# A hybrid decoder block with expert retrieval: gathered rows paced over the whole dense stage, three buffers for split rows, one-hots moved to ScalarE, unsplit meta columns

## The chip, the cores and the metric

The kernel runs on one core of one Trainium2 chip. The metric is the device time of one execution in microseconds (us), the median of the runs. Engines are named as in the profile: PE is TensorE, DVE is VectorE, ACT is ScalarE, POOL is GpSimd and SP is SyncE; PEld is the load of weights into PE.

## The reference

512 tokens of width 1024, with 16 learned meta tokens in front, go through one layer in float32:

```
h = concat(meta, x)
h = h + hybrid_mixer(rmsnorm(h))      # stick-breaking attention and gated linear attention
h = h + peer_ffn(rmsnorm(h))          # product-key retrieval of experts
return rmsnorm(h)[:, 16:]

def peer_ffn(hn, ...):                # 8 heads, 128 keys a half, top 16, 128 x 128 experts
    s1, s2 = q[:, :, 0] @ sub_keys1, q[:, :, 1] @ sub_keys2
    v1, i1 = top_k(s1, 16);  v2, i2 = top_k(s2, 16)
    sc, pos = top_k(v1[:, None] + v2[None, :], 16)
    e = i1 * 128 + i2 at pos;  g = softmax(sc)          # 128 experts a token
    act = gelu(expert_u[e] . hn)
    y = sum over the 128 experts of g * act * expert_v[e]
```

So each token picks 128 of 16384 experts, each a row of 1024 numbers in `expert_u` and one in `expert_v`.

## The kernel before

**Stages.** `front` norms the input and projects it (w_in in chunks of 256 columns) into queries, keys, values and gates, and runs both attentions; `mid` applies w_out and the second norm and projects the retrieval queries. The projections use float32 operands split into a high and a low part (`hilo`, lines 174 and 175: the high part by ACT, the low part by DVE) and three matmuls per product (`mm3`, lines 179 to 181). The 16 meta columns of keys and gates are products of their own with 16 moving columns, into `pz`, from the same split weights `wh` and `wl` and the split activations `hnh` and `hnl`.

**Look stage.** The tokens lie in four blocks of 128. Three of them (DENSE) are computed against all 16384 experts, the fourth (block 3, GATHER) only against its own. A u row (`u_row`) takes 128 experts: 0.5 MB of `expert_ut` into `uf`, split into `uh` and `ul`, 24 matmuls against the 384 dense tokens, Gelu into `ge`. Between u rows a queue of generators runs the retrieval. For each block `topk` finds experts and gates: scores by PE, copied to `sc` by ACT (line 626), then MAX8, FIND_INDEX8 and MATCH_REPLACE8 on DVE, and two lookups, each of 16 products (line 683) and one sum (line 687). For each dense block `spread` turns them into gates over all experts: 32 steps of four tokens, each with a one-hot `B` (line 769, DVE), a product `Am` of two smaller one-hots (line 771, POOL), four matmuls (line 775, PE), and an eviction `st` with a step of 16 elements (line 776, ACT). `st` goes out to `Gd` in memory. The jobs stand in the order topk 0, spread 0, topk 1, spread 1, topk 2, spread 2, topk 3. The `ge` of the pairs of u rows computed here goes out to `Ad` (23 pairs).

**Dense stage.** The rows go on in pairs. For the pairs that are not yet computed, two more u rows come first (41 pairs); the others are read back from `Ad`. Each pair then takes two v rows (`v_operands`, `v_block`): 0.5 MB of `expert_v` into the same `uf` buffers, split into `uh` and `ul` as above, `ge` times the gates `gt` (1.5 MB of `Gd` for every eight rows) and split into `wh` and `wl`, and 18 matmuls of 512 columns that add up in six banks `acc`. Beside them runs block 3 (`gathered`): 128 times a gather of `expert_u` rows by an indirect DMA from POOL (line 715) into one of six buffers `gu` and a product with accumulation on DVE (line 722), then Gelu on ACT, and 128 gathers of `expert_v` that DVE adds to `y` (line 733).

**What sets the order.** Both stages are paced by a queue: each u row pays 4.2 units, each v row 4.1, times a rate (RATES: 1.3 in the look stage, 0.62 in the dense stage), and each step of a generator costs what it yields (1.0 for four tokens of `spread`, 1.3 for a gathered row). From the program a scheduler then fixes one order for each engine, which the engine follows. The tile pools set the buffers: 4 for `uf`, 2 for `uh` and `ul`, 6 for `gu`, 3 for `B` and `Am`, 6 banks for `sx`.

Of the kernel before, what the change touches and what calls it, by code (L numbers as in the profile page):

```python
# [21 lines left out]
D = 1024  # L22
# [12 lines left out]
GB = 6  # L35
GEB = 5
UF = 4


RATES = (1.3, 0.62)  # L40
LNEXP = "natural_log_exp_and_others"

SEGS = []
# [17 lines left out]
def build(tc, d, out):  # L61
# [121 lines left out]
    def proj(src, c, jobs, act, cols=256, halves=(0, 1)):  # L183


        for half in halves:
            wf = wp.tile([128, 4, 256], F32, name="wf", bufs=WF)
            nc.sync.dma_start(wf[:, :, :cols], src[c, :, half * 4:half * 4 + 4, :cols])
            wh = wp.tile([128, 4, 256], F32R, name="wh", bufs=2)
            wl = wp.tile([128, 4, 256], F32R, name="wl", bufs=2)  # L190
            hilo(wh[:, :, :cols], wl[:, :, :cols], wf[:, :, :cols])
            for (o, kind, w0, w1, t0, t1, fst) in jobs:
                for k in range(4):
                    kt = half * 4 + k
                    a = act(kt, t0, t1)
                    w = (wh[:, k, w0:w1], wl[:, k, w0:w1])
                    l, r = (w, a) if kind == 'f' else (a, w)
                    mm3(o, l, r, kt == 0 and fst, kt == KT - 1)
# [4 lines left out]
                 b % 2 == 0) for b in range(NB)]  # L203

    win = d["w_in"]
    oTh = wp.tile([128, KT, W], F32R, name="oTh")
    oTl = wp.tile([128, KT, W], F32R, name="oTl")

    def front():
# [24 lines left out]
        for q in range(2):  # L234
            for x, n, col in rows:
                t = bank(next(tags))
                for k in range(4):
                    T.transpose(t[:, k * n:(k + 1) * n], x[:, (4 * q + k) * 128:(4 * q + k + 1) * 128], ident[:n, :n])
                for k in range(4):
                    kt = 4 * q + k  # L240
                    hi = hnh[:, kt, col:col + n]
                    A.activation(hi, t[:, k * n:(k + 1) * n], AF.Copy, scale=g1[:, kt:kt + 1])
                    V.scalar_tensor_tensor(hnl[:, kt, col:col + n], t[:, k * n:(k + 1) * n], g1[:, kt:kt + 1],
                                           hi.bitcast(F32), op0=OP.mult, op1=OP.subtract)
        consts_b()

        def act(kt, a, b):
# [2 lines left out]
        def feat(c, meta=None):  # L250
            outs = [pj(), pj()]
            jobs = [(outs[m], 'f', m * 128, (m + 1) * 128, NM, E, True) for m in range(2)]
            if meta is not None:
                jobs += [(meta[:, m * 16:(m + 1) * 16], 'f', m * 128, (m + 1) * 128, 0, NM, m == 0) for m in range(2)]
            proj(win, c, jobs, act)
            return outs

# [134 lines left out]

        def gates_():
            p, pm = pj(), pz()
            proj(win, 12, [(p[:66], 'f', 0, 66, NM, E, True), (pm[:66, :16], 'f', 0, 66, 0, NM, True)], act, cols=66)
            A.activation(glr[:, NM:], p[:16], AF.Copy)
            A.activation(glr[:, :NM], pm[:16, :16], AF.Copy)

# [212 lines left out]
    def topk(blk):  # L611
# [63 lines left out]
        df = mp.tile([128, NH, TK], F32, name="df")  # L675
        V.tensor_copy(df[:, :, 0:1], cs[:, :, 0:1])
        V.tensor_sub(df[:, :, 1:], cs[:, :, 1:], cs[:, :, :TK - 1])
        terms = sc.rearrange("p s h k -> p (s h k)").rearrange("p (a h k) -> p a h k", a=TK, h=NH)

        def lookup(dst, src, keys, op, vals):  # L680

            for a in range(TK):
                V.scalar_tensor_tensor(terms[:, a], src, float(keys[a]), vals[:, :, a:a + 1].to_broadcast([128, NH, TK]),  # L683
                                       op0=op, op1=OP.mult)
                if a % 4 == 3:
                    yield 0.9
            V.tensor_reduce(dst, terms.rearrange("p a h k -> p (h k) a"), op=OP.add, axis=AX.X)

        yield from lookup(cs.rearrange("p h k -> p (h k)"), fp, STARTS, OP.is_ge, df)
        ci = mp.tile([128, 2, NH, TK], I32, name="ci")  # L690
# [44 lines left out]
    def spread(blk, nb=3):  # L735

        pt = bank("sx")
        for i, src in enumerate((sels[blk][:, 0], sels[blk][:, 1], gates[blk])):  # L740
            T.transpose(pt[:, i * 128:(i + 1) * 128], src, ident)
        iT = bp.tile([128, 4, 128], F32, name="iT")
        V.tensor_copy(iT[:, :3], pt[:, :384].rearrange("p (a b) -> p a b", a=3))
        ii = bp.tile([128, 2, 128], I32, name="ii")
        V.tensor_copy(ii[:, 0], pt[:, :128])
        V.tensor_scalar(ii[:, 1], ii[:, 0], 7, None, op0=OP.bitwise_and)
        V.tensor_scalar(ii[:, 0], ii[:, 0], 3, None, op0=OP.logical_shift_right)
        V.tensor_copy(iT[:, 0], ii[:, 0])
        V.tensor_copy(iT[:, 3], ii[:, 1])
        yield 1.5  # L750
        sh = [128, 4, 128]
        io4 = io128.unsqueeze(1).to_broadcast(sh)
        for tb in range(128 // TT):
            st = bp.tile([128, 128, TT], F32, name="st", bufs=2)
            tc_ = slice(tb * TT, (tb + 1) * TT)
            ohu = bp.tile([128, TT, 16], F32, name="ohu", bufs=2)
            V.tensor_tensor(ohu, io128[:, :16].unsqueeze(1).to_broadcast([128, TT, 16]),
                            iT[:, 0, tc_].unsqueeze(2).to_broadcast([128, TT, 16]), op=OP.is_equal)
            ohl = bp.tile([128, TT, 8], F32, name="ohl", bufs=2)
            V.tensor_tensor(ohl, io128[:, :8].unsqueeze(1).to_broadcast([128, TT, 8]),  # L760
                            iT[:, 3, tc_].unsqueeze(2).to_broadcast([128, TT, 8]), op=OP.is_equal)
            V.tensor_tensor(ohl, ohl, iT[:, 2, tc_].unsqueeze(2).to_broadcast([128, TT, 8]), op=OP.mult)  # L762
            yield 1.2
            for t4 in range(TT // 4):
                p = bank("sx")
                c_ = slice(tb * TT + t4 * 4, tb * TT + t4 * 4 + 4)
                l_ = slice(t4 * 4, t4 * 4 + 4)
                B = bp.tile(sh, F32, name="B", bufs=nb)
                V.tensor_tensor(B, io4, iT[:, 1, c_].unsqueeze(2).to_broadcast(sh), op=OP.is_equal)  # L769
                Am = bp.tile(sh, F32, name="Am", bufs=nb)  # L770
                P.tensor_tensor(Am.rearrange("p t (u l) -> p t u l", l=8),  # L771
                                ohu[:, l_].unsqueeze(3).to_broadcast([128, 4, 16, 8]),
                                ohl[:, l_].unsqueeze(2).to_broadcast([128, 4, 16, 8]), op=OP.mult)
                for j in range(4):
                    T.matmul(p[:, j * 128:(j + 1) * 128], B[:, j], Am[:, j], start=True, stop=True)  # L775
                A.activation(st[:, :, t4 * 4:t4 * 4 + 4].rearrange("p i t -> p t i"),
                             p.rearrange("p (t i) -> p t i", t=4), AF.Copy)
                yield 1.0
            nc.scalar.dma_start(Gd[128 // TT * DENSE.index(blk) + tb], st)


# [32 lines left out]
    def u_row(i1, dst):  # L814

        uf = du.tile([128, KT, 128], F32, name="uf", bufs=UF)
        uh = du.tile([128, KT, 128], F32R, name="uh", bufs=2)
        ul = du.tile([128, KT, 128], F32R, name="ul", bufs=2)
        nc.sync.dma_start(uf, d["expert_ut"][i1])
        hilo(uh, ul, uf)  # L820
        pu = pj()[:, :DT]
        for kt in range(KT):
            mm3(pu, (uh[:, kt], ul[:, kt]), (xDh[:, kt, :DT], xDl[:, kt, :DT]), kt == 0, kt == KT - 1)
        A.activation(dst, pu, AF.Gelu)
# [4 lines left out]
    def v_operands(i1, ge):  # L829
        nonlocal gt, gti  # L830
        vf = du.tile([128, D], F32, name="uf", bufs=UF)
        nc.sync.dma_start(vf, d["expert_v"][i1 * 128:(i1 + 1) * 128, :])
        vh = du.tile([128, D], F32R, name="uh", bufs=2)
        vl = du.tile([128, D], F32R, name="ul", bufs=2)
        hilo(vh, vl, vf)
        if i1 // IC != gti:
            gti = i1 // IC
            gt = dp.tile([128, TB, IC, TT], F32, name="gt", bufs=2)
            nc.sync.dma_start(gt, Gd[:, :, gti * IC:gti * IC + IC, :].rearrange("a p i t -> p a i t"))
        g3 = ge.rearrange("p (a t) -> p a t", t=TT)  # L840
        V.tensor_tensor(g3, g3, gt[:, :, i1 % IC, :], op=OP.mult)
        wh = dp.tile([128, DT], F32R, name="wh2", bufs=2)
        wl = dp.tile([128, DT], F32R, name="wl2", bufs=2)
        hilo(wh, wl, ge)
        return wh, wl, vh, vl
# [101 lines left out]
    for blk in GATHER:  # L947
        final(blk, ys[blk])
    for i, blk in enumerate(DENSE):
        hb = du.tile([128, D], F32, name="uh", bufs=2)  # L950
        nc.sync.dma_start(hb, hd[blk])
        final(blk, hb, i)
    pool_close("du")
# [60 lines left out]
```

## Time and profile before

| | |
|---|---|
| runs | 1907.78, 1908.71, 1917.06 us; median 1908.71 |
| profiled execution | 1921.35 us; its span 1919.5 us |
| mean granted clock of PE | 0.938 |
| busy: PE | 1668.2 us (87% of the span) |
| busy: DVE | 1246.5 us (65%) |
| busy: ACT | 697.8 us (36%) |
| busy: POOL | 523.9 us (27%) |
| DMA | 374.40 MB, mean 195 GB/s |

Busy shares are means over stages with different limits. A row of the windows gives a stretch, its length, and the busy time and number of instructions of PE, PEld, DVE, ACT and POOL in it, then the granted clock, the share of the 16 DMA engines and GB/s. A row of the timeline gives start, duration, engine, line and operation; "x2" merges neighbours, and the brackets give the idle time of the engine before it with what ended it. A row of the groups gives busy time and mean ns of one, then the idle time before them. A row of the waits gives who waited for whom: us in total, times, longest.

### The profile page before, as it was taken

To read this page: it belongs to the slowest core of one execution; us is meant where nothing else is said; L and a number is where in the kernel's file an instruction comes from. 1 tells how busy PE (TensorE), PEld (TensorE's weight loads), DVE (VectorE), ACT (ScalarE), POOL (GpSimd) and SP (SyncE) were. 2 spreads that over 40 slices of the span, in tenths; PEclk is the share of its full clock that TensorE was granted. 3 is DMA by queue.
4 is the path that set the end of the run, shared out by engine and by line. 5 is a ranking of instruction groups with operands and counts; after the bars stand their busy time and mean duration, and the time that the engine had idled before them with its cause. 6 is when DMAs were issued, how large, how long until landed. Compare 5 with 4: busy or idle time off the path is not lost.

```text
span 1919.5 us, 23858 instructions
## 1 busy us (share of the span) xinstructions
PE 1668.2 (87%) x8783; PEld 1448.7 (75%) x8783; DVE 1246.5 (65%) x2436; ACT 697.8 (36%) x1039; POOL 523.9 (27%) x407
## 2 busy tenths in 40 slices
PE   6999989988787897886889897978888999999995
PEld 4874777967676786776678787867777888887884
DVE  4111284546968979978788786768776964454554
ACT  4245363433443452532223232222222333333342
POOL 0013000000350530713555564555545610000000
PEclk9899989989999998988899998989898999999998
DMA  5110111332343343437998988988897964387643
GB/s 165 59 37 1 64 33 60 110 114 91 124 158 114 148 179 102 176 132 262 358 350 310 356 314 301 329 295 320 294 319 268 387 230 154 131 258 232 205 156 106
DMA packets 148596, 374.40 MB, mean 195 GB/s; under 512 B 12768, under 2 KB 65136, under 8 KB 145408
## 3 DMA queue, kind: packets, MB, share of 16 engines
q1 hardware_dynamic: 103696, 201.29, 31.6%
q0 software_dynamic: 36864, 134.23, 18.9%
q10 hardware_dynamic: 7920, 37.36, 4.9%
q8 instruction: 69, 1.13, 0.3%
q14 instruction: 47, 0.39, 0.1%
HBM read 334.41 MB, written 38.40 MB: 194 GB/s over the span
## 4 chain that ended last, share of the span: by engine, by line
PE 44%; DVE 20%; issue 15%; DMA 10%; POOL 6%; ACT 4%; DVEq 0%; SPq 0%; POOLq 0%; ACTq 0%
PE pj L181 7%; PE pj L179 7%; PE pj L180 7%; POOL gu L715 6%; PE acc L180 5%; PE acc L179 5%; PE acc L181 5%; DMA uf<-expert_ut 4%; DVE ul L175 3%; DVE B L769 3%; DMA gu<-expert_v,idx 2%; PE sx L775 2%; DMA gu<-expert_u,idx 2%; DVE y L733 1%; DVE sc L683 1%
## 5 line engine op out<-in xcount | busy, mean ns | idle before, releaser
L174 ACT ACTIVATE uh<-uf 128x1024 fp32r<-128x1024 f32 x256 | 269.6, 1053 | 509.3 <-PE pj L180 391.2
L181 PE MATMUL pj<-xDh,ul 128*128 128x384 f32 x1024 | 373.6, 366 | 78.3 <-DVE ul L175 78.3
L179 PE MATMUL pj<-xDh,uh 128*128 128x384 f32 x1024 | 373.3, 365 | 52.1 <-ACT uh L174 39.5
L175 DVE TENSOR_TENSOR ul<-uf,uh 128x1024 fp32r<-128x1024 f32 x256 | 321.3, 1255 | 146.1 <-ACT uh L174 143.2
L180 PE MATMUL pj<-xDl,uh 128*128 128x384 f32 x1024 | 367.8, 359 | 0.0
L179 PE MATMUL acc<-uh,wh 128*128 128x512 f32 x768 | 303.9, 396 | 11.0 <-ACT wh L174 11.0
L180 PE MATMUL acc<-ul,wh 128*128 128x512 f32 x768 | 305.0, 397 | 4.0 <-DVE ul L175 4.0
L181 PE MATMUL acc<-uh,wl 128*128 128x512 f32 x768 | 303.8, 396 | 0.4 <-DVE wl L175 0.4
L181 PEld LDWEIGHTS pj<-xDh,ul 128*128 128x128 f32 x1024 | 211.5, 207 | 90.5 <-DVE ul L175 90.4
L771 POOL TENSOR_TENSOR Am<-ohu,ohl 128x512 f32<-128x512 f32 x96 | 133.3, 1411 | 499.7 <-DVE ohl L762 442.6
L179 PEld LDWEIGHTS pj<-xDh,uh 128*128 128x128 f32 x1024 | 212.4, 207 | 61.4 <-ACT uh L174 43.2
L715 POOL DMA_INDIRECT gu<-expert_u,idx x128 | 184.6, 1442 | 229.8 <-DVE gu L722 76.4
L180 PEld LDWEIGHTS pj<-xDl,uh 128*128 128x128 f32 x1024 | 211.5, 207 | 1.4
L715 POOL DMA_INDIRECT gu<-expert_v,idx x128 | 179.4, 1402 | 120.3 <-DVE y L733 54.0
L722 DVE SCALAR_TENSOR_TENSOR gu<-gu,xn 128x1024 f32<-128x1024 f32 x128 | 152.5, 1219 | 63.4 <-DMA gu<-expert_u,idx 56.8
L174 ACT ACTIVATE wh<-ge 128x384 fp32r<-128x384 f32 x128 | 67.0, 524 | 320.7 <-PE acc L180 271.4
L179 PEld LDWEIGHTS acc<-uh,wh 128*128 128x128 f32 x768 | 144.6, 188 | 45.6 <-ACT wh L174 11.9
L180 PEld LDWEIGHTS acc<-ul,wh 128*128 128x128 f32 x768 | 144.6, 188 | 40.1 <-DVE ul L175 6.9
L181 PEld LDWEIGHTS acc<-uh,wl 128*128 128x128 f32 x768 | 144.5, 188 | 35.5 <-DVE wl L175 1.1
L733 DVE SCALAR_TENSOR_TENSOR y<-gu,act,y 128x1024 f32<-128x1024 f32 x128 | 164.5, 1285 | 2.4 <-DMA gu<-expert_v,idx 1.2
L175 DVE TENSOR_TENSOR wl<-wf,wh 128x1024 fp32r<-128x1024 f32 (+1 forms) x42 | 49.8, 1186 | 167.0 <-ACT wh L174 167.0
L775 PE MATMUL sx<-Am,B 128*128 128x128 f32 x768 | 105.7, 289 | 30.2 <-DVE B L769 25.1
(313 smaller groups left out, 2282.5 us busy)
## 6 DMA issues: line engine op xcount, KB each, us to landing
uf<-expert_ut SPq DMA_DIRECT2D x128, 512.0 KB
uf<-expert_v SPq DMA_DIRECT2D x128, 512.0 KB
gt<-Gd SPq DMA_DIRECT2D x17, 1536.0 KB
Gd<-st ACTq DMA_DIRECT2D x24, 1024.0 KB
wf<-w_in SPq DMA_DIRECT2D x24, 512.0 KB
Ad<-ge ACTq DMA_DIRECT2D x23, 384.0 KB
ge<-Ad SPq DMA_DIRECT2D x23, 384.0 KB
wf<-w_out SPq DMA_DIRECT2D x8, 512.0 KB
```

Source lines behind the costliest of these rows:

```text
L174: A.activation(hi, src, AF.Copy)
L175: V.tensor_tensor(lo, src, hi.bitcast(F32), op=OP.subtract)
L179: T.matmul(outp, lh, rh, start=first, stop=False, skip_group_check=True)
L180: T.matmul(outp, lh, rl, start=False, stop=False, skip_group_check=True)
L181: T.matmul(outp, ll, rh, start=False, stop=last, skip_group_check=True)
L683: V.scalar_tensor_tensor(terms[:, a], src, float(keys[a]), vals[:, :, a:a + 1].to_broadcast([128, NH, TK]), op0=op, op1=OP.mult)
L715: P.indirect_dma_start(out=u, out_offset=None, in_=d[table], in_offset=bass.IndirectOffsetOnAxis(ap=col, axis=0))
L722: V.scalar_tensor_tensor(u, u, 1.0, xns[blk], op0=OP.mult, op1=OP.mult, accum_out=acts[blk][:, k:k + 1]))
L733: V.scalar_tensor_tensor(y, u, acts[blk][:, k:k + 1], y, op0=OP.mult, op1=OP.add))
L769: V.tensor_tensor(B, io4, iT[:, 1, c_].unsqueeze(2).to_broadcast(sh), op=OP.is_equal)
L771: P.tensor_tensor(Am.rearrange("p t (u l) -> p t u l", l=8), ohu[:, l_].unsqueeze(3).to_broadcast([128, 4, 16, 8]), ohl[:, l_].unsqueeze(2 ...
L775: T.matmul(p[:, j * 128:(j + 1) * 128], B[:, j], Am[:, j], start=True, stop=True)
```

## The change

Five things change. The rate of the dense stage goes from 0.62 to 0.43 and that of the look stage from 1.3 to 1.2, with three of four spread steps yielding 0.5 in place of 1.0. `uh` and `ul` get three buffers each. Of the one-hots `B` three of four are made by ACT: the absolute difference of a row of numbers and the token's index, in four activations with the negated index as bias, and one Relu of 1 minus it. The lookups lay out their terms so that the sum reads neighbours, and the products write with a step of 16 elements. The products of the meta columns take the unsplit weights `wf` and an unsplit copy `hnm` of the 16 columns, in one float32 matmul in place of three.

```diff
-RATES = (1.3, 0.62)
+UH = 3
+RATES = (1.2, 0.43)
@@ proj
                     kt = half * 4 + k
+                    if kind == 'm':
+                        T.matmul(o, wf[:, k, w0:w1], hnm[:, kt], start=kt == 0 and fst, stop=kt == KT - 1,
+                                 skip_group_check=True)
+                        continue
@@ front
+                    if n == NM:
+                        A.activation(hnm[:, kt], t[:, k * n:(k + 1) * n], AF.Copy, scale=g1[:, kt:kt + 1])
...
-                jobs += [(meta[:, m * 16:(m + 1) * 16], 'f', m * 128, (m + 1) * 128, 0, NM, m == 0) for m in range(2)]
+                jobs += [(meta[:, m * 16:(m + 1) * 16], 'm', m * 128, (m + 1) * 128, 0, NM, m == 0) for m in range(2)]
@@ topk
-        terms = sc.rearrange("p s h k -> p (s h k)").rearrange("p (a h k) -> p a h k", a=TK, h=NH)
+        terms = sc.rearrange("p s h k -> p (s h k)").rearrange("p (h k a) -> p h k a", a=TK, h=NH)
...
-                V.scalar_tensor_tensor(terms[:, a], src, float(keys[a]), vals[:, :, a:a + 1].to_broadcast([128, NH, TK]),
+                V.scalar_tensor_tensor(terms[:, :, :, a], src, float(keys[a]), vals[:, :, a:a + 1].to_broadcast([128, NH, TK]),
...
-            V.tensor_reduce(dst, terms.rearrange("p a h k -> p (h k) a"), op=OP.add, axis=AX.X)
+            V.tensor_reduce(dst, terms.rearrange("p h k a -> p (h k) a"), op=OP.add, axis=AX.X)
@@ spread
+        nT = bp.tile([128, 128], F32, name="nT")
+        V.tensor_scalar(nT, iT[:, 1], -1.0, None, op0=OP.mult)
...
-                V.tensor_tensor(B, io4, iT[:, 1, c_].unsqueeze(2).to_broadcast(sh), op=OP.is_equal)
+                if t4 == TT // 4 - 1:
+                    V.tensor_tensor(B, io4, iT[:, 1, c_].unsqueeze(2).to_broadcast(sh), op=OP.is_equal)
+                else:
+                    for j in range(4):
+                        t = tb * TT + t4 * 4 + j
+                        A.activation(B[:, j], io128, AF.Abs, bias=nT[:, t:t + 1])
+                    A.activation(B, B, AF.Relu, scale=-1.0, bias=1.0)
...
-                yield 1.0
+                yield 1.0 if t4 == TT // 4 - 1 else 0.5
@@ u_row and v_operands
-        uh = du.tile([128, KT, 128], F32R, name="uh", bufs=2)
-        ul = du.tile([128, KT, 128], F32R, name="ul", bufs=2)
+        uh = du.tile([128, KT, 128], F32R, name="uh", bufs=UH)
+        ul = du.tile([128, KT, 128], F32R, name="ul", bufs=UH)
```

The look stage now computes 22 pairs of u rows ahead instead of 23. In the new kernel the lines lie some 10 to 18 further down: line 776 is 794, and the one-hots on ACT are lines 786 and 787.

On ACT, early in the first spread phase, the order before is (st is the eviction, L174 the split of a u row, L824 its Gelu):

```order
L776 ACTIVATE st<-sx 128x4x128 x4
L779 DMA Gd<-st 128x2048
L776 ACTIVATE st<-sx 128x4x128 x5
L779 DMA Gd<-st 128x2048
L824 ACTIVATE ge<-pj 128x384
L776 ACTIVATE st<-sx 128x4x128 x4
```

In the same place the order now is (B is the one-hot, L786 its four differences, L787 its Relu):

```order
L786 ACTIVATE B<-io_80,nT 128x128 x5
L787 ACTIVATE B<-B 128x512
L786 ACTIVATE B<-io_80,nT 128x128 x4
L787 ACTIVATE B<-B 128x512
L794 ACTIVATE st<-sx 128x4x128
L786 ACTIVATE B<-io_80,nT 128x128 x3
L794 ACTIVATE st<-sx 128x4x128
L787 ACTIVATE B<-B 128x512
L842 ACTIVATE ge<-pj 128x384
```

Between two evictions there now stand some four to five one-hot activations, and an eviction stands one or two one-hots behind its own.

On DVE, in the dense stage, a pair of rows while block 3 adds up `y` reads before:

```order
L733 SCALAR_TENSOR_TENSOR y<-gu,act_96,y 128x1024
L841 TENSOR_TENSOR ge<-ge,gt 128x384
L175 TENSOR_TENSOR wl_9761<-ge,wh_9760 128x384
L175 TENSOR_TENSOR ul<-uf,uh 128x1024
L733 SCALAR_TENSOR_TENSOR y<-gu,act_96,y 128x1024 x2
L175 TENSOR_TENSOR wl_9796<-ge,wh_9795 128x384
L175 TENSOR_TENSOR ul<-uf,uh 128x1024
```

And now, in a pair that gathers `expert_u` (L731 is line 722 of before, L859 is line 841):

```order
L859 TENSOR_TENSOR ge<-ge,gt 128x384
L176 TENSOR_TENSOR wl_11153<-ge,wh_11152 128x384
L731 SCALAR_TENSOR_TENSOR gu,act_97<-gu,xn_3114 128x1024
L176 TENSOR_TENSOR ul<-uf,uh 128x1024
L731 SCALAR_TENSOR_TENSOR gu,act_97<-gu,xn_3114 128x1024 x2
L176 TENSOR_TENSOR wl_11188<-ge,wh_11187 128x384
L176 TENSOR_TENSOR ul<-uf,uh 128x1024
```

The products of gathered rows still stand between the splits, so that a split waits for the gather ahead of it; there are fewer of them in a pair, and they go on beside the first v rows that read `Ad`.

More of the change, by code (lines that the diff above doesn't have):

```diff
@@ L205, in build @@
     win = d["w_in"]
+    hnm = pp.tile([128, KT, NM], F32, name="hnm")
     oTh = wp.tile([128, KT, W], F32R, name="oTh")
@@ L394, in gates_ @@
             p, pm = pj(), pz()
-            proj(win, 12, [(p[:66], 'f', 0, 66, NM, E, True), (pm[:66, :16], 'f', 0, 66, 0, NM, True)], act, cols=66)
+            proj(win, 12, [(p[:66], 'f', 0, 66, NM, E, True), (pm[:66, :16], 'm', 0, 66, 0, NM, True)], act, cols=66)
             A.activation(glr[:, NM:], p[:16], AF.Copy)
@@ L832, in v_operands @@
         nc.sync.dma_start(vf, d["expert_v"][i1 * 128:(i1 + 1) * 128, :])
-        vh = du.tile([128, D], F32R, name="uh", bufs=2)
-        vl = du.tile([128, D], F32R, name="ul", bufs=2)
+        vh = du.tile([128, D], F32R, name="uh", bufs=UH)
+        vl = du.tile([128, D], F32R, name="ul", bufs=UH)
         hilo(vh, vl, vf)
@@ L949, in build @@
     for i, blk in enumerate(DENSE):
-        hb = du.tile([128, D], F32, name="uh", bufs=2)
+        hb = du.tile([128, D], F32, name="uh", bufs=UH)
         nc.sync.dma_start(hb, hd[blk])
```

## The prediction

> **What bounds the kernel now.** I read the windows by stage first. Each row gives a stretch, its length, the busy time of PE, weight load, DVE, ACT and POOL, then the granted clock, the DMA share and GB/s.
>
> ```profile
> 0.00:450.00 450.00, 404.52 (x2505) 325.54 (x2507) 173.12 (x315) 196.55 (x367) 26.63 (x55) 0.95 0.21 70
> 450.00:885.00 435.00, 344.22 (x2047) 322.84 (x2046) 380.87 (x1227) 185.49 (x222) 133.30 (x96) 0.92 0.38 139
> 885.00:1555.00 670.00, 577.88 (x2677) 513.71 (x2676) 518.53 (x651) 187.71 (x264) 364.01 (x256) 0.92 0.90 324
> 1555.00:1690.00 135.00, 135.00 (x679) 121.77 (x678) 57.63 (x68) 46.60 (x64) 0.00 (x0) 1.00 0.50 160
> 1690.00:1897.00 207.00, 206.58 (x884) 164.86 (x882) 105.93 (x146) 76.24 (x105) 0.00 (x0) 1.00 0.61 194
> ```
>
> The front (0 to 450) is PE's. In the look stage (450 to 885) VectorE leads with 381 of 435 us. The dense stage (885 to 1897) has two faces: while block 3 gathers (all 256 POOL instructions) PE is idle for 92 us and its clock is 0.92; afterwards PE is full at clock 1.00. So the tail shows what a row costs when nothing disturbs it. The timeline gives that cost: 24 matmuls of a u row lie between the last two lines here, 22 of a v row between the first two.
>
> ```profile
> 1039.67 0.39 PE L180 MATMUL acc<-ul,wh 128*128 128x512 f32 x1
> 1044.80 0.39 PE L181 MATMUL acc<-uh,wl 128*128 128x512 f32 x1
> 1045.03 0.34 PE L179 MATMUL pj<-xDh,uh 128*128 128x384 f32 x1
> 1049.19 0.34 PE L179 MATMUL pj<-xDh,uh 128*128 128x384 f32 x1
> ```
>
> A u row is 4.16 us, a v row 18 x 5.13 / 22 = 4.20 us. The dense stage of before holds 128 - 46 = 82 u rows and 128 v rows: 341 + 538 = 879 us. It takes 1012, so 133 us are lost, all while gathers run. The waits of 885 to 1555, a group, and one place in the timelines and the chain (with the first and the last of seven gt loads) say how:
>
> ```profile
> ACT uh L174 <- DMA uf<-expert_ut: 57.0, 9, 9.5
> DVE gu L722 <- DMA gu<-expert_u,idx: 56.8, 20, 5.4
> PE pj L181 <- DVE ul L175: 40.7, 17, 5.0
> PE pj L179 <- ACT uh L174: 35.1, 7, 6.7
> PE acc L179 <- ACT wh L174: 11.0, 2, 9.4
> L722 DVE SCALAR_TENSOR_TENSOR gu<-gu,xn 128x1024 f32<-128x1024 f32 x128 | 152.5, 1219 | 63.4 <-DMA gu<-expert_u,idx 56.8 <-issue 6.6
> 975.65 0.38 SPq L839 DMA_DIRECT2D gt<-Gd  x1
> 1057.44 0.38 SPq L839 DMA_DIRECT2D gt<-Gd  x1
> 1060.33 22.65 DMA uf<-expert_ut
> 1084.15 1.23 DVE L175 TENSOR_TENSOR ul<-uf,uh 128x1024 fp32r<-128x1024 f32 x1 [8.54 <-ACT uh L174]
> 1086.84 1.68 POOL L715 DMA_INDIRECT gu<-expert_u,idx  x1 [10.42 <-DVE y L733]
> 1104.97 1.23 DVE L722 SCALAR_TENSOR_TENSOR gu<-gu,xn 128x1024 f32<-128x1024 f32 x1 [4.17 <-DMA gu<-expert_u,idx]
> 1487.11 0.38 SPq L839 DMA_DIRECT2D gt<-Gd  x1
> ```
>
> The 1.5 MB gt load goes out among the gathers, and the u row issued behind it needs 22.65 us to land. VectorE stands 8.54 us at that row's ul, and behind it in its queue stand products of gathered rows whose buffers POOL needs, so POOL stops for 10.42 us. Twenty us later the missing gathers stop VectorE again, and with it the next ul and PE. This repeats at the gt loads. It isn't plain lack of bandwidth, since near the end PE stays nearly full while more is moved:
>
> ```profile
> 1500.00:1520.00 20.00, 18.86 (x95) 16.67 (x94) 17.72 (x18) 7.45 (x10) 12.10 (x9) 1.00 1.03 405
> 1520.00:1540.00 20.00, 20.00 (x100) 17.73 (x99) 19.89 (x21) 6.23 (x9) 14.94 (x10) 1.00 1.02 393
> ```
>
> **The change, part by part.** *Gathers and buffers.* A gather costs 1.3 units. A pair of rows of each kind paid (2 x 4.2 + 2 x 4.1) x 0.62 = 10.3 units, 7.9 gathers; at 0.43 it pays 7.1, 5.5 gathers. Block 3 then takes all 42 fresh pairs and about 19 v rows of the tail instead of 32 pairs. At the ideal 16.7 us a pair, 4 rows of 0.524 MB, a quarter of gt (0.39) and 5.5 gathers make 5.4 MB, 321 GB/s: no more than the 324 that the stage moves now, and under 393 to 405. VectorE's work on gathers falls by 2.4 x 1.22 (L722) = 2.9 us a pair. The third pair of split buffers lets the split run one more row ahead, 4.2 us; that is as long as most of the stalls (76 us in 24 waits of PE before L181 and L179, 3.2 each). Undisturbed, the stage now has 84 u rows (one more pair comes over from look): 349 + 538 = 887, 8 more than before. Of the loss of 133 I put about 25 on the opening (the 11.0 and the 6.7 above, with the slow clock behind them), which stays, and the other 108 on the seven gt loads that gathers met afterwards, 15.4 each. In the new order on SP's queue the gathers meet about 11. I take 2 us each, since both the slack and the pace improve: loss 25 + 22 = 47. Dense stage: 8 - 133 + 47 = **-78 us**. Bounds: 1 each (-89) and the old 15.4 each (+69).
>
> *One-hots.* In a spread phase and in the top-k phase behind it:
>
> ```profile
> 635.00:711.00 76.00, 64.08 (x437) 60.42 (x436) 59.93 (x67) 41.94 (x47) 43.89 (x32) 0.96 0.43 162
> 711.00:763.00 52.00, 39.12 (x186) 36.62 (x185) 51.16 (x258) 14.85 (x21) 0.00 (x0) 0.87 0.35 119
> L769 DVE TENSOR_TENSOR B<-io,iT 128x512 f32<-128x512 f32 x96 | 102.3, 1082 | 28.6 <-PE sx L775 28.5
> 329.16 0.68 ACT L497 ACTIVATE kd<-bc,nb 128x128 f32<-128x128 f32 x2
> 131.99 1.15 ACT L301 ACTIVATE az<-az 128x512 f32<-128x512 f32 x2
> ```
>
> The spread phase has no full engine (PE 64, VectorE 60 of 76), the top-k phase is VectorE's (51 of 52). 24 of 32 one-hots per phase leave VectorE: 24 x 1.08 = 26 us. On ScalarE one takes four 128-column activations with a bias pointer and one of 512. L497 is the nearest row: two in 0.68 with the second lasting 0.39, so 0.29 from start to start; L301 gives 0.52 likewise. 4 x 0.29 + 0.52 = 1.68, times 24 = 40. ScalarE gets 42 + 40 = 82 us, more than the phase is long, and its queue is in order: each eviction st (L776) and each split uh now stands behind one-hots, and PE's next one-hot product waits for the Relu. At 92% filling a phase takes 88 us, 12 more; three phases **+36**. The scores of the next top-k are copied by ScalarE behind the last st, so VectorE's free time can't be used by the next phase. Bounds: 76 (the activations overlap better than L497, or +0) and 97 (+63; filled as PE is now, 84%). [...]
>
> *Lookups.* The sums now read in line, the 128 products write with a step of 64 B.
>
> ```profile
> L687 DVE TENSOR_REDUCE sel<-sc 128x128 f32<-128x2048 f32 x4 | 15.2, 3791 | 0.0
> L683 DVE SCALAR_TENSOR_TENSOR sc<-bb,fi 128x128 f32<-128x128 f32 x64 | 13.3, 284 | 0.0
> L776 ACT ACTIVATE st<-sx 128x512 f32<-128x512 f32 x96 | 96.9, 1066 | 47.0 <-PE sx L775 45.1 <-ACT st L776 0.9 <-ACT ge L824 0.4
> L626 ACT ACTIVATE sc<-sx 128x512 f32<-128x512 f32 x16 | 8.5, 603 | 0.9 <-PE sx L622 0.9
> ```
>
> Twice the 1.22 of L722 bounds an in-line sum of 2048 at 2.4 us, 1.35 less; eight make -11. For the writes L776 against L626 is the nearest pair, the same 512 columns with and without a 64 B step: 0.90 ns an element more, 0.116 us for 128, +15 for 128 products at most, 0 at least. I take half, +8. By the order, VectorE has three u rows fewer to split in the first three top-k phases (20 for 23), -4. Sum **-7**, from -15 to 0. [...]
>
> *Meta columns.* 56 products of three become 56 of the unsplit kind.
>
> ```profile
> 59.28 0.26 PE L180 MATMUL pz<-hnl,wh 128*128 128x16 f32 x1
> 59.39 0.26 PE L181 MATMUL pz<-hnh,wl 128*128 128x16 f32 x1
> 214.92 0.51 PE L404 MATMUL pz<-glr,wgu 16*128 16x16 f32 x4
> 23.03 0.53 ACT L242 ACTIVATE hnh<-po,g 128x16 fp32r<-128x16 f32 x2
> ```
>
> 0.11 us from start to start, so 168 take 19 us. L404's two calls show four matmuls at the same pace, so 112 take 12.5: -6, in a stretch where PE is full. Eight copies hnm of some 0.26 us (L242) stand in ScalarE's queue ahead of the first weights, +2. Sum **-4**, from -6 to +6. [...] L404 shows two matmuls to a call.
>
> PE now reads wf itself, so its buffer comes free later and SP's next weight load goes out later; with three buffers and the DMA at 0.21 in the front I cost that at nothing (without this cover, up to a 0.5 MB load in each of seven chunks). nT is one small VectorE instruction per block, hidden in a spread phase where VectorE has air; otherwise under 1 us.
>
> **Sum.** The profiled execution took 1921.35 us, span 1919.5. -78 + 36 - 7 - 4 = -53, so 1868. The median of the runs shown, 1908.71, is 0.9934 of the profiled one: **1856 us**.
>
> **Rivals.** (1) *ScalarE's work disappears* in a phase that had room on every engine, and phases stay at 76: 36 less, 1832, or 1820 as a median. For it: ScalarE waited 45 us for PE before st. Against it: 82 us don't fit into 76.
> (2) *The stall belongs to the gt load, not to the pace.* Then the gathers, stretched over the stage, meet 11 loads instead of 7, at 15.4 us each: +69 in place of -78, 2015, median 2002, slower. It decides at 25 + 11x: from x = 6.8 us a load the gain is gone. Against it: the two windows of 393 and 405 GB/s; for it: each of the six earlier loads shows the stall.
> (3) *ScalarE's queue stalls in order*: every st waits for its own product, eight matmuls at L404's pace, 0.9 us, 32 times: phases of 110 us, +102 in place of +36: 1934, median 1921, slower. It decides at phases of 106. Against it: the order lets one or two one-hots stand between a one-hot and its st.
>
> **Chances.** My sum 0.62; (1) 0.16; (2) 0.16, half of it between 5.9 and 7.7 us a load, which is no change; (3) 0.06, half of it no change. A measurement can tell about 0.5%, 9.5 us. Faster 0.78, same 0.11, slower 0.11. The range starts at (1) with a load at 1 us, 1809, and ends at a load at 6 us, 1900.
>
> **What would show it.** Right: PE near 100% in the gather stretch at clock 1.00, POOL's last gather some 80 us from the end of the products; spread phases of 85 to 90 us with ScalarE above 80; sums near 2.4 us. Wrong: PE idle 3 to 5 us behind each gt load as before, or spread phases of 76 or of over 100.

## The result and the profile after

The changed kernel takes 1838.37 us (median of 4 runs, 1836.94 to 1841.80), the kernel before 1908.24 beside it: ratio 0.9628, 95% interval 0.9595 to 0.9662. Its profiled execution took 1841.80 us, span 1840.0.

The windows of the changed kernel by stage (length, PE, weight load, DVE, ACT, POOL busy, then clock, DMA share, GB/s):

```profile
0.00:437.60 437.60, 393.46 (x2468) 315.87 (x2470) 172.84 (x315) 197.82 (x376) 26.57 (x55) 0.95 0.21 70
437.60:900.20 462.60, 342.65 (x1967) 321.14 (x1964) 265.41 (x1154) 292.83 (x576) 111.60 (x96) 0.86 0.36 129
898.00:1603.00 705.00, 691.88 (x3461) 623.79 (x3460) 550.06 (x699) 241.69 (x339) 329.12 (x234) 0.99 0.93 325
1603.00:1700.00 97.00, 81.16 (x324) 63.57 (x323) 68.21 (x84) 26.64 (x36) 36.64 (x22) 0.92 0.89 307
1700.00:1817.00 117.00, 117.00 (x501) 94.05 (x500) 66.59 (x90) 45.26 (x64) 0.00 (x0) 1.00 0.57 182
```

The front became 13 us shorter, the look stage 29 longer (VectorE fell from 381 to 265 us there, ScalarE rose from 185 to 293), and the dense stage 88 shorter. While fresh u rows run beside gathers, PE now has 692 of 705 us at clock 0.99 where it had 578 of 670 at 0.92. Of the 29 us that PE still loses in the dense stage, 13 lie at the opening (before 1000 us) and 16 in 1603 to 1700, where the last gathers meet the pairs read back from `Ad`.

The waits of the dense stage (us in total, times, longest), then, from SP's timeline, the first and the last gt load among the fresh u rows:

```profile
DVE ge L859 <- DMA ge<-Ad: 48.4, 18, 9.4
DVE gu L731 <- DMA gu<-expert_u,idx: 9.0, 5, 5.9
ACT uh L175 <- DMA uf<-expert_ut: 2.6, 3, 1.4
PE acc L182 <- DVE wl L176: 15.8, 5, 8.0
PE acc L180 <- ACT wh L175: 12.6, 2, 6.9
PE pj L182 <- DVE ul L176: 0.6, 1, 0.6
```

```profile
1002.39 0.38 SPq L857 DMA_DIRECT2D gt<-Gd  x1
...
1537.48 0.38 SPq L857 DMA_DIRECT2D gt<-Gd  x1
```

ScalarE waited 57.0 us for rows of `expert_ut` before and 2.6 now; VectorE waited 56.8 us for gathered rows and 9.0 now; PE's 75.8 us before u rows are 0.6. Nine gt loads go out between 1002 and 1538 without a stall. Of PE's waits before v rows the 12.6 us are the opening and the 15.8 us the tail.

The three spread phases, then the groups, then the waits of the look stage:

```profile
488.00:581.00 93.00, 66.84 (x413) 62.32 (x413) 23.55 (x47) 77.66 (x165) 36.98 (x32) 0.85 0.36 135
629.00:721.00 92.00, 67.61 (x416) 63.08 (x415) 26.24 (x46) 77.89 (x165) 36.79 (x32) 0.85 0.36 136
769.00:854.00 85.00, 63.99 (x414) 59.72 (x413) 25.08 (x45) 75.83 (x164) 37.82 (x32) 0.88 0.35 134
```

```profile
L794 ACT ACTIVATE st<-sx 128x512 f32<-128x512 f32 x96 | 100.0, 1046 | 31.5 <-PE sx L793 30.9
L786 ACT ACTIVATE B<-io,nT 128x128 f32<-128x128 f32 x288 | 91.8, 387 | 0.0
L787 ACT ACTIVATE B<-B 128x512 f32<-128x512 f32 x72 | 45.0, 624 | 0.2
L692 DVE SCALAR_TENSOR_TENSOR sc<-bb,fi 128x128 f32<-128x128 f32 x64 | 15.1, 387 | 0.0
L696 DVE TENSOR_REDUCE sel<-sc 128x128 f32<-128x2048 f32 x4 | 9.1, 2278 | 0.0
```

```profile
PE sx L793 <- ACT B L787: 65.5, 44, 2.9
```

ScalarE is now the busiest engine of these phases, but not full (77 of 92 us): it waits 30.9 us in all for PE before `st`, and PE waits 65.5 us for ScalarE's Relu. A timeline of 629 to 721 shows the loop:

```profile
658.08 1.05 PE L793 MATMUL sx<-Am,B 128*128 128x128 f32 x8
659.17 1.03 ACT L794 ACTIVATE st<-sx 128x512 f32<-128x512 f32 x1 [1.12 <-PE sx L793]
660.00 0.62 ACT L787 ACTIVATE B<-B 128x512 f32<-128x512 f32 x1
660.77 2.02 PE L793 MATMUL sx<-Am,B 128*128 128x128 f32 x16 [1.64 <-ACT B L787]
661.94 1.04 ACT L794 ACTIVATE st<-sx 128x512 f32<-128x512 f32 x1 [0.15 <-PE sx L793]
```

The Relu at 660.00 stands behind an eviction, which waits for a product; the next product waits for that Relu.

At the end the loads of the residual rows `hd`, before and then in the changed kernel:

```profile
1896.24 1.02 SPq L951 DMA_DIRECT2D uh<-hd  x2
1906.61 0.32 SPq L951 DMA_DIRECT2D uh<-hd  x1
```

```profile
1816.01 8.05 SPq L969 DMA_DIRECT2D uh<-hd  x2
1824.64 0.37 SPq L969 DMA_DIRECT2D uh<-hd  x1
```

`hb` lives in the `uh` buffers (the last hunk of the diff). With two of them, the third block's load went out 9.7 us after the last product (1896.9), when the first block was done; with three it goes out with the last product (1824.4). I had not counted this.

### The profile page after: what moved, and what is told of

Same layout as the page of the kernel before. It is cut to its first block, busy times and chain, and to the rows that moved or that the text cites. A ratio compares the mean times of both kernels' runs of the same rounds, so it can differ in the third digit from the quotient of the medians.

```text
span 1840.0 us, 24030 instructions
## 1 busy us (share of the span) xinstructions
PE 1631.4 (89%) x8727; PEld 1421.9 (77%) x8727; DVE 1131.6 (61%) x2367; ACT 810.1 (44%) x1407; POOL 503.9 (27%) x407
## 4 chain that ended last, share of the span: by engine, by line
PE 67%; DVE 14%; ACT 9%; DMA 6%; issue 3%; POOL 1%; SPq 0%; ACTq 0%; DVEq 0%; POOLq 0%
PE pj L180 10%; PE pj L182 10%; PE pj L181 10%; PE acc L182 8%; PE acc L180 8%; PE acc L181 8%; PE sx L793 4%; ACT st L794 3%; DMA ge<-Ad 3%; ACT B L786 2%; DVE ul L176 2%; ACT B L787 1%; DVE sc L692 1%; DMA uf<-expert_v 1%; DVE iu L649 1%
## 5 line engine op out<-in xcount | busy, mean ns | idle before, releaser
L176 DVE TENSOR_TENSOR ul<-uf,uh 128x1024 fp32r<-128x1024 f32 x256 | 315.4, 1233 | 166.6 <-ACT uh L175 164.4
L182 PE MATMUL pj<-xDh,ul 128*128 128x384 f32 x1024 | 352.5, 344 | 35.1 <-DVE ul L176 35.1
L180 PE MATMUL pj<-xDh,uh 128*128 128x384 f32 x1024 | 354.3, 346 | 9.3 <-ACT ge L842 8.0
L181 PE MATMUL pj<-xDl,uh 128*128 128x384 f32 x1024 | 350.7, 342 | 0.0
L182 PE MATMUL acc<-uh,wl 128*128 128x512 f32 x768 | 308.0, 401 | 15.8 <-DVE wl L176 15.8
L180 PE MATMUL acc<-uh,wh 128*128 128x512 f32 x768 | 307.3, 400 | 12.6 <-ACT wh L175 12.6
L789 POOL TENSOR_TENSOR Am<-ohu,ohl 128x512 f32<-128x512 f32 x96 | 111.6, 1172 | 547.9 <-ACT B L786 306.4
L182 PEld LDWEIGHTS pj<-xDh,ul 128*128 128x128 f32 x1024 | 197.4, 193 | 40.0 <-DVE ul L176 39.8
L180 PEld LDWEIGHTS pj<-xDh,uh 128*128 128x128 f32 x1024 | 197.7, 193 | 14.4 <-ACT ge L842 10.7
L181 PEld LDWEIGHTS pj<-xDl,uh 128*128 128x128 f32 x1024 | 197.7, 193 | 1.7
L793 PE MATMUL sx<-Am,B 128*128 128x128 f32 x768 | 127.2, 328 | 71.2 <-ACT B L787 65.5
L793 PEld LDWEIGHTS sx<-Am,B 128*128 128x128 f32 x768 | 117.2, 237 | 83.2 <-issue 43.0
L731 DVE SCALAR_TENSOR_TENSOR gu<-gu,xn 128x1024 f32<-128x1024 f32 x128 | 153.9, 1219 | 9.0 <-DMA gu<-expert_u,idx 9.0
```

What stands on the lines that cost most here:

```text
L176: V.tensor_tensor(lo, src, hi.bitcast(F32), op=OP.subtract)
L180: T.matmul(outp, lh, rh, start=first, stop=False, skip_group_check=True)
L181: T.matmul(outp, lh, rl, start=False, stop=False, skip_group_check=True)
L182: T.matmul(outp, ll, rh, start=False, stop=last, skip_group_check=True)
L731: V.scalar_tensor_tensor(u, u, 1.0, xns[blk], op0=OP.mult, op1=OP.mult, accum_out=acts[blk][:, k:k + 1]))
L789: P.tensor_tensor(Am.rearrange("p t (u l) -> p t u l", l=8), ohu[:, l_].unsqueeze(3).to_broadcast([128, 4, 16, 8]), ohl[:, l_].unsqueeze(2 ...
```

## The experiments

The table gives for each run the median and ratio, and the stages of its profiled execution: front to the first copy of scores, look stage to the last lookup sum, dense stage to the last product of `acc`, the end, and PE's idle time in the dense stage. The marks are read from the timelines. The kernel before, measured beside each group of runs, had medians of 1911.94 to 1912.49 there, so a difference of two medians can be a few us off what the ratios give.

| run | median us | ratio to before, 95% interval | front | look | dense | end | PE idle |
|---|---|---|---|---|---|---|---|
| before | 1908.24 | | 451.0 | 433.9 | 1012.0 | 22.6 | 92.4 |
| changed | 1838.37 | 0.9628 [0.9595, 0.9662] | 437.6 | 462.6 | 924.2 | 15.6 | 29.0 |
| e_pace | 1828.17 | 0.9558 [0.9518, 0.9599] | 453.1 | 431.7 | 917.8 | 21.8 | 33.3 |
| e_uh | 1854.64 | 0.9687 [0.9644, 0.9730] | 453.4 | 421.7 | 964.8 | 15.4 | 67.4 |
| e_meta | 1895.60 | 0.9904 [0.9874, 0.9934] | 436.7 | 437.0 | 1004.0 | 21.7 | 82.9 |
| e_look | 1906.81 | 0.9969 [0.9951, 0.9986] | 455.1 | 424.7 | 1004.3 | 22.3 | 83.3 |
| e_act | 1977.48 | 1.0342 [1.0314, 1.0369] | 452.2 | 494.5 | 1002.8 | 22.0 | 86.3 |
| e_mix | 1909.71 | 0.9979 [0.9963, 0.9996] | 446.4 | 434.0 | 1005.1 | 22.1 | 89.8 |
| a_dve | 1778.77 | 0.9297 [0.9257, 0.9336] | 436.9 | 406.3 | 918.3 | 15.7 | 32.0 |
| a_one | 1788.91 | 0.9347 [0.9322, 0.9373] | 434.9 | 420.8 | 915.0 | 15.5 | 37.1 |
| e_nb | 1841.93 | 0.9639 [0.9605, 0.9673] | 437.9 | 460.7 | 926.2 | 15.6 | 29.8 |
| a_48 | 1764.48 | 0.9238 [0.9216, 0.9261] | 437.8 | 405.7 | 902.0 | 15.4 | 21.3 |
| a_u2 | 1797.27 | 0.9418 [0.9389, 0.9448] | 434.9 | 416.1 | 921.2 | 22.4 | 34.0 |
| a_11 | 1769.24 | 0.9274 [0.9243, 0.9305] | 435.0 | 417.9 | 897.9 | 15.7 | 39.6 |

Where a part is untouched, profiles differ by a few us: the front 451.0 to 455.1 in five, the dense stage 1002.8 to 1012.0 in five, with that of before at the top. So against the usual 1004 the dense stage gained 80 us, not 88.

**Pace alone (e_pace)**, the kernel before with one number changed:

```diff
-RATES = (1.3, 0.62)
+RATES = (1.3, 0.43)
```

> The kernel before with the rate of the dense stage at 0.43 alone (split buffers stay at two). If the pace of the gathers is what stalls PE behind each gt load, the dense stage falls from 1012 us to about 930 and the total by some 75 us, to 1833. If the stalls belong to the gt load and to the short supply of split rows, each of some 11 loads keeps its 10 to 15 us, the dense stage stays between 1000 and 1060, and the total is 1900 or more.

Its windows among fresh u rows and just behind them:

```profile
940.00:1570.00 630.00, 629.12 (x3164) 568.01 (x3163) 500.85 (x628) 220.12 (x308) 286.61 (x209) 1.00 0.91 321
1570.00:1685.00 115.00, 98.73 (x400) 76.96 (x399) 83.34 (x102) 33.11 (x47) 43.37 (x28) 0.96 0.94 336
```

PE misses 1 us of 630, and the dense stage is as short as with the whole change. More gt loads meet gathers there and none stalls: the stall belonged to the pace, not to the load. Alone this edit takes 4.4% off, at least as much as the whole change with its 3.7% (the intervals just touch).

**Third split buffer alone (e_uh)**, before with `bufs=3` for `uh` and `ul`:

```diff
-        uh = du.tile([128, KT, 128], F32R, name="uh", bufs=2)
-        ul = du.tile([128, KT, 128], F32R, name="ul", bufs=2)
+        uh = du.tile([128, KT, 128], F32R, name="uh", bufs=3)
+        ul = du.tile([128, KT, 128], F32R, name="ul", bufs=3)
... (the same for the v rows, and bufs=3 for hb)
```

> The kernel before with three split buffers alone (rate stays at 0.62). If one more row of supply covers the stalls (3.2 us a wait on average against 4.2 us of cover), PE's idle time in the gather stretch falls from 92 to about 30 us and the total by 70 to 80. If the pace is the cause, VectorE still stands at late gathers, and the total falls by less than 25 us.

```profile
940.00:1483.00 543.00, 502.17 (x2424) 447.27 (x2423) 460.03 (x576) 169.58 (x239) 335.56 (x231) 0.96 0.96 353
```

Neither expectation came true. At the old pace the buffer takes 39 us off the usual 1004 of the dense stage, where the pace alone takes 86; PE's idle time falls to 67 us and not to 30 (PE has 502 of 543 us). ScalarE still waits 74.5 us for rows of `expert_ut` (57.0 before; no such wait stands in the list of e_pace). The rest of the gain is some 12 us in the look stage and 7 at the end.

**Two buffers beside the slow pace (a_u2)**, a_dve (below) with `UH = 2`:

```diff
-UH = 3
+UH = 2
```

> All one-hots on VectorE, dense rate 0.43, but two buffers for split rows again instead of three, beside 1779 with three. Theory A (with the slow pace the third buffer does nothing in the dense stage, and it is worth the 12 us in the look stage that it brought alone): dense stage within 3 us of 918, look stage 418, 1790. Theory B (it matters in neither): 1779. Theory C (it is needed in the dense stage too): above 1795.

Theory A holds for the dense stage (921.2 against 918.3) and the look stage (+10); the 7 us by which the end grew again make up most of the rest. Beside the slow pace the buffer pays in the look stage and at the end only.

**Meta columns alone (e_meta)**, before with the `'m'` products and the `hnm` copies of the diff:

```diff
+                    if kind == 'm':
+                        T.matmul(o, wf[:, k, w0:w1], hnm[:, kt], start=kt == 0 and fst, stop=kt == KT - 1,
+                                 skip_group_check=True)
+                        continue
... (hnm and the two job lists as in the diff)
```

> The kernel before with the meta columns in unsplit products alone. By counting matmuls it is 56 x 0.11 = 6 us, less 2 for the copies: total down by 4 us, 1904. If the front's 13 us come from this edit alone, as the full-width runs of 24 narrow matmuls are each followed by 3.4 us of half clock in the kernel before and by none in the changed one, the total falls by 13 us, to 1895, and the clock of the front shows no half-speed stretch between 60 and 90 us.

The front is 14 to 18 us shorter than the five with the old products, where I had 4. The profile of before has a reason that I had passed over, in three windows; the same three in e_meta stand at clock 1.00.

```profile
62.00:66.00 4.00, 4.00 (x11) 3.12 (x12) 1.23 (x1) 0.97 (x1) 0.00 (x0) 0.57 0.13 40
72.00:76.00 4.00, 4.00 (x12) 3.13 (x11) 1.23 (x1) 1.38 (x5) 0.00 (x0) 0.57 0.18 57
82.00:87.00 5.00, 5.00 (x16) 3.97 (x15) 1.23 (x1) 1.19 (x2) 0.00 (x0) 0.66 0.31 102
```

The granted clock falls, with PE busy throughout, each time behind a run of 24 narrow products. The front of before has six such runs, and four of them are followed by a fall; the runs at 88.7 and 232.3 us are not (the last section sets them side by side).

**Narrow products in shorter runs (e_mix)**, before with the same products in another order:

```diff
-            jobs = [(outs[m], 'f', m * 128, (m + 1) * 128, NM, E, True) for m in range(2)]
-            if meta is not None:
-                jobs += [(meta[:, m * 16:(m + 1) * 16], 'f', m * 128, (m + 1) * 128, 0, NM, m == 0) for m in range(2)]
+            jobs = []
+            for m in range(2):
+                jobs.append((outs[m], 'f', m * 128, (m + 1) * 128, NM, E, True))
+                if meta is not None:
+                    jobs.append((meta[:, m * 16:(m + 1) * 16], 'f', m * 128, (m + 1) * 128, 0, NM, m == 0))
```

> The kernel before, with the meta products of the two halves of a chunk put apart, each behind the wide products of its half: the same matmuls, but the narrow ones in runs of 12 (1.3 us) instead of 24 (2.6 us). Theory A (the granted clock falls to half for 3.4 us after each run of 24 narrow matmuls, as the front of before shows at 62.3, 72.5 and 82.8, and this was part of the 13 us that the front became shorter): no fall of the clock there, and the front 4 to 6 us shorter, time 1903. Theory B (the clock has another cause, such as the weight loads): the fall stays, time 1909 within 3.

```profile
62.00:66.00 4.00, 4.00 (x25) 3.52 (x24) 1.23 (x1) 0.89 (x2) 0.00 (x0) 1.00 0.28 89
72.00:76.00 4.00, 4.00 (x25) 3.48 (x24) 0.74 (x1) 0.00 (x0) 0.00 (x0) 1.00 0.40 131
82.00:87.00 5.00, 5.00 (x33) 4.47 (x33) 0.00 (x0) 1.47 (x6) 0.00 (x0) 1.00 0.16 52
```

The three falls are gone and the front is 5 to 9 us shorter, without a product less. By the ratio it is 4 us (0.4 to 7). Four falls of 3.4 us, at 0.43 us a product instead of 0.23, come to some 6 us.

**Lookups alone (e_look)**, before with the new layout of the terms:

```diff
-        terms = sc.rearrange("p s h k -> p (s h k)").rearrange("p (a h k) -> p a h k", a=TK, h=NH)
+        terms = sc.rearrange("p s h k -> p (s h k)").rearrange("p (h k a) -> p h k a", a=TK, h=NH)
```

> The kernel before with the new layout of the lookup terms alone. By the rows of the changed kernel a product takes 388 instead of 284 ns and a sum 2.28 instead of 3.79 us: 128 products +13.6, eight sums -11.9, so +2 us in all, and the look stage within 3 us of the 434 of before. [...] If the layout itself were what took 28 us out of the look stage (theory B, beside theory A that the freed VectorE and the third buffer did), the time is below 1890.

The +2 that I had worked out from the rows of the changed kernel missed: the look stage lost 9 us, and the ratio gives 6 (3 to 9), near the forecast of 7. Theory B, 28 us, is out. I had added up durations. The timelines of VectorE, of before and of e_look, show why that fails:

```profile
484.94 3.30 DVE L683 SCALAR_TENSOR_TENSOR sc<-fp,df 128x128 f32<-128x128 f32 x16
488.37 3.73 DVE L687 TENSOR_REDUCE cs<-sc 128x128 f32<-128x2048 f32 x1
```

```profile
489.03 3.78 DVE L683 SCALAR_TENSOR_TENSOR sc<-fp,df 128x128 f32<-128x128 f32 x16
492.84 2.29 DVE L687 TENSOR_REDUCE cs<-sc 128x128 f32<-128x2048 f32 x1
```

A product lasts 0.39 instead of 0.28 us, but instructions in a row overlap: sixteen take 3.78 instead of 3.30. So a lookup loses 0.48 and gains 1.44, about 1.0 us eight times.

**One-hots on ScalarE alone (e_act)**, before with the `else` branch of the diff, its paces and yields kept:

```diff
-                V.tensor_tensor(B, io4, iT[:, 1, c_].unsqueeze(2).to_broadcast(sh), op=OP.is_equal)
+                if t4 == TT // 4 - 1:
+                    V.tensor_tensor(B, io4, iT[:, 1, c_].unsqueeze(2).to_broadcast(sh), op=OP.is_equal)
+                else:
...
+                        A.activation(B[:, j], io128, AF.Abs, bias=nT[:, t:t + 1])
+                    A.activation(B, B, AF.Relu, scale=-1.0, bias=1.0)
```

> The kernel before with three of four one-hots on ScalarE alone, its paces and yields kept but for that. Theory A (a one-hot on ScalarE costs the spread phase some 15 to 18 us each, and the 28 us that the look stage grew by are this price less what the third buffer and the rest brought): look stage +45 to +56, the time 1955 to 1970. Theory B (the price is the 29 us seen, nothing compensates): 1938. Theory C (the phases only grow because the third buffer lets more splits crowd ScalarE): within 15 us of before.

```profile
505.00:599.00 94.00, 72.66 (x463) 67.53 (x462) 26.20 (x46) 79.76 (x168) 39.05 (x32) 0.91 0.36 136
649.00:753.00 104.00, 75.02 (x438) 70.11 (x437) 25.90 (x46) 79.88 (x167) 36.57 (x32) 0.82 0.33 122
```

61 us more, above even theory A's 56: this edit alone makes the kernel 3.4% slower. VectorE's work in a phase falls from 60 to 26 us, and nothing uses what it leaves.

**The changed kernel with all one-hots on VectorE (a_dve)**:

```diff
-RATES = (1.2, 0.43)
+RATES = (1.3, 0.43)
... (both branches of the changed kernel go, and in their place:)
+                V.tensor_tensor(B, io4, iT[:, 1, c_].unsqueeze(2).to_broadcast(sh), op=OP.is_equal)
...
-                yield 1.0 if t4 == TT // 4 - 1 else 0.5
+                yield 1.0
```

> The changed kernel with all one-hots back on VectorE (line of before, each step yielding 1.0, look rate 1.3); pace 0.43, three buffers, lookups and meta columns stay. If ScalarE bounds the spread phases of the changed kernel, they return from 82 to 76 us and with the 1.1 us a one-hot less work the total falls by 15 to 30 us, to 1808 to 1823. If the move to ScalarE carried part of the gain, the total rises above 1838.

```profile
487.00:561.00 74.00, 61.55 (x437) 58.83 (x437) 64.42 (x72) 41.56 (x46) 46.95 (x32) 0.98 0.47 174
608.00:677.00 69.00, 61.77 (x444) 59.44 (x442) 61.51 (x71) 41.17 (x46) 43.46 (x32) 0.98 0.52 193
```

60 us faster than the changed kernel, twice what I expected at most; 56 of them lie in the look stage, which has 23 pairs here for 22. Spread phases take 69 to 74 us with PE and VectorE nearly full.

**One of four on ScalarE (a_one)**, the changed kernel with yields and rates as in a_dve, and:

```diff
-                if t4 == TT // 4 - 1:
+                if t4 != 1:
```

> The changed kernel with one of four one-hots on ScalarE instead of three (eight a phase, 14 us of ScalarE work there, which then has 56 of some 74 us), against 1779 with none and 1838 with three. If ScalarE's filling is what costs (theory A), it has room for eight and the phases stay near 74: 1775 to 1785, perhaps a gain of some us since VectorE is left with 48. If each one-hot costs by the chain it adds (ScalarE's queue in order, PE waiting for the Relu; theory B), a third of the price is paid: 1795 to 1800.

A spread phase and the top-k phase behind it:

```profile
486.00:566.00 80.00, 77.32 (x534) 75.14 (x533) 54.16 (x66) 57.87 (x95) 48.19 (x32) 0.98 0.54 197
566.00:610.00 44.00, 17.81 (x90) 16.87 (x89) 43.99 (x253) 9.29 (x13) 0.00 (x0) 0.69 0.18 64
```

Between the theories, and it doesn't decide: the order drew u rows out of the top-k phases into the spread phases, where PE is now full (77 of 80 us), and left PE empty behind them (18 of 44).

**More buffers (e_nb)**, the changed kernel with:

```diff
-    def spread(blk, nb=3):
+    def spread(blk, nb=5):
```

> The changed kernel with five buffers for B and Am in place of three. In its spread phases ScalarE is busy for 77 of some 91 us, and PE waits 65.5 us in all for the Relu. Theory A (ScalarE's queue stands in order among one-hots and evictions that wait for PE and POOL; with more buffers the one-hots run ahead of their use): phases of 82 to 85, the time 1815 to 1825. Theory B (ScalarE's own work and the chain from Abs to Relu to product to eviction are the length, buffers or not): 1838 within 6.

```profile
629.00:721.00 92.00, 67.95 (x406) 62.79 (x404) 31.05 (x42) 77.11 (x165) 37.69 (x32) 0.83 0.35 132
```

Theory B: the time is that of the changed kernel, and the look stage takes 460.7 us for 462.6. The number of these buffers is not what holds ScalarE at 77 of 92 us. Whether another order of its queue would wasn't tried.

**A little faster pace (a_48)**, a_dve with:

```diff
-RATES = (1.3, 0.43)
+RATES = (1.3, 0.48)
```

> All one-hots on VectorE, dense rate 0.48 instead of 0.43, beside 1779 for the same at 0.43. At 0.43 the stretch of fresh u rows has no PE stall at all, and the first 117 us of the tail lose 14 us, with the last 27 gathers beside gt loads and reads of Ad. Theory A (the loss is those gathers meeting the reads of Ad in the tail, and the pace has room): gathers end with the u rows, the tail loses 2 us, 1767. Theory B (at 0.48 the rows stall behind gathers again, as at 0.62, where 59 us were lost): 1779 to 1795.

```profile
895.00:1490.00 595.00, 592.61 (x2966) 534.14 (x2967) 499.90 (x629) 210.65 (x295) 320.54 (x219) 1.00 0.96 343
1490.00:1590.00 100.00, 96.51 (x446) 81.25 (x445) 72.94 (x86) 32.81 (x47) 26.05 (x18) 1.00 0.88 298
```

Theory A: the gathers end at 1544, 14 us behind the last u row instead of 113, and PE's idle time falls by 11 us. This is the fastest kernel of the study, 74 us under the changed one.

**More u rows ahead (a_11)**, a_dve with:

```diff
-RATES = (1.3, 0.43)
+RATES = (1.1, 0.43)
```

> All one-hots on VectorE, look rate 1.1 instead of 1.3, so that 27 pairs of u rows instead of 23 are computed in the look stage and the dense stage has eight fresh u rows fewer (33 us at 4.16). PE is idle there for some 60 of 406 us. Theory A (the idle PE takes the rows, and only VectorE's splits of some 1.4 us each lengthen its full top-k phases): 8 x 1.4 = 11 of the 33 given back, 1757. Theory B (the rows stand in each engine's fixed order between the steps of the retrieval and lengthen the look stage by their whole length): 1779 or more.

The look stage grew by 12 us, as theory A had it, but the dense stage gained 20 instead of 33: with fewer u rows the last gathers reach 192 us into the tail (1470 to 1662), and PE idles 8 us more. Neither theory's time came out (1757, or 1779 and more), and by the intervals it can't be told from a_dve.

## Why the prediction was right, and which terms were off

The time, 1838, lies within the range and 18 under the forecast of 1856. By the profiles the stages moved by -13.4, +28.7, -87.8 and -7.0, -79.5 in all; my sum was -53.

*Gathers and buffers* (-78; measured -80 against the usual 1004). The mechanism and the size held, but I gave the gain to two causes. Pace alone brings it, and beside it the third buffer adds 3 us there. The price of 2 us a gt load was too high, while the last gathers, which end 132 us before the last product and not 80, cost 14 to 16 us among the reads of `Ad` that I had not priced. A row quoted in the prediction gives a likely reason for the old loss: VectorE 19.89 of 20 us busy. At 0.62 a pair needs 4 x 1.22 for splits, 2 x 1.10 for gates and 7.9 x 1.30 for gathered rows, 17.4 us by durations. As time in which VectorE was busy it is some 16 (468.98 us for 230 gathers in 940 to 1543 of before), against PE's 16.7, so next to nothing was left to catch up after a stall; at 0.48 it is 14, the 84% of a_48's window. That last step is argued; that 0.48 runs without loss among fresh rows, and 0.62 doesn't, is shown.

*One-hots* (+36; measured +56 to +61, inside the bound of 63). ScalarE's work was right (77 us for 82), its filling of 92% was not: 83 to 89%, with evictions waiting for PE and PE for the Relu. And without the edit a phase would not have stayed at 76 us but become 69 to 74. e_act (look stage 61 us longer) and a_dve (60 us faster than the changed kernel) both speak against the move. An activation of 128 columns with a bias pointer lasts 0.39 us in the trace (L786), and five in a row take 1.54 us, 0.29 from start to start, as the prediction had it from L497; phases are 85 to 93 us, for the 88 of the forecast.

*Lookups* (-7; measured -9 in the look stage, -6 by the ratio). The sum was right by luck in one part: the writes cost +4, not +8, and the fewer u splits were not needed. The step in the writes costs little: 0.23 us from start to start with it (e_look), 0.20 without (before; 15 steps in 3.78 less 0.39, and in 3.30 less 0.28), so 0.03 us a product and not the 0.116 that I had taken from ScalarE's eviction as the most. The sums take 2.28 us, near the 2.4 of the forecast.

*Meta columns* (-4; measured -14 to -18). The fewer products stand for the 6 us that I had: 24 split matmuls take 2.6 us in the trace of before, 16 unsplit ones 1.7 in that of the changed kernel, which has 112 of them (L198, two to a product) for 168. No run shows the +6 us at which the range ended; these paces give 6 us less. The clock gives 5 to 9 more by the front of e_mix, which no step of mine had. What is left, some 3 us, stays open.

*The end* (no term; -7): the third buffer for `hb`.

So the look stage's +29, which my terms +36 and -7 seem to hit, is two errors that cancel: one-hots cost 20 us more, and the third buffer brought 10 to 12 there that I hadn't given it.

*Rivals.* The first is out: phases grew. The second is out: nine loads pass without a stall (e_pace and the changed kernel). The third has the right mechanism, PE waiting 65.5 us for the Relu, but not its price: phases of 90 us on average, not 110. Against the old phases of 76 that is 42 us of its 102; against those of a_dve, 71 on average, 57.

## What to carry to other kernels

Before work is moved to an engine with free time, look whose queue it joins: here it stood in order between evictions that wait for PE and products that wait for it, it made each phase longer, and the time that VectorE got free went unused. Background transfers are worth a pace that fits the stage beside them: here the best one tried left VectorE, which consumes them, 16% of its time (a_48), and ended just where the fresh u rows did; 0.62 was too fast and 0.43 a little too slow. A change in several parts is worth taking apart: without the one-hots the others bring 7.0% (a_dve), and the one-hots take 60 us of it back.

## What the runs showed of the hardware that was not expected

The granted clock of PE fell while PE was never idle (busy for 30.00 us of 40 to 70, in before). A piece of PE's timeline before: the last narrow product of a run, and the wide ones behind it.

```profile
61.73 0.26 PE L181 MATMUL pz<-hnh,wl 128*128 128x16 f32 x1
...
63.33 0.63 PE L180 MATMUL pj<-hnl,wh 128*128 128x512 f32 x1
63.75 0.63 PE L181 MATMUL pj<-hnh,wl 128*128 128x512 f32 x1
...
66.04 0.40 PE L181 MATMUL pj<-hnh,wl 128*128 128x512 f32 x1
```

24 products of 16 columns, 2.6 us of them, are followed here by 3.4 us at half the clock (0.43 us from start to start instead of 0.23). Not every such run is. In the clock record of this trace the stretches of half clock behind such runs last 3.41 us each and start at multiples of 3.41 us from one another (62.29, 72.53, 82.77 and 226.13 us). With the trace divided into stretches of 3.41 us in step with these starts, the four runs have 2.60, 2.54, 2.11 and 2.42 us in the stretch right ahead of the fall. The runs at 88.7 and 232.3 us have at most 1.69 and 1.98 us in one stretch, and no fall follows them. None follows the six runs of 16 unsplit matmuls in the changed kernel either (1.7 us), nor do the runs of 12 in e_mix (1.3 us) bring one between 50 and 120 us, where the clock is 1.00. That the time within one stretch tells the runs apart is my reading of these few; why the clock falls was not shown.

Durations in the records of VectorE overlap by 0.08 us for 128 columns, and by 0.16 when the write is strided (0.28 against 0.20 in before, 0.39 against 0.23 in e_look): the price of an instruction in a row is read from start to start.
